# Output stage of a hybrid DeltaNet and attention layer: the residual gate moved from the weights to the results, and the first two units run side by side

## The chip, the cores and the metric

One core of a Trainium2 chip runs the whole layer. The metric is the device time of one execution in microseconds (us). TensorE (PE) multiplies, VectorE (DVE), ScalarE (ACT) and GpSimd (POOL) do the elementwise work, and SyncE (SP) and ScalarE issue the DMAs.

## The reference, cut to what matters

```python
def _merge(ya, yb, ga, gb, w_proj_a, w_proj_b, w_out):
    y = jax.nn.sigmoid(ga) * (ya @ w_proj_a) + jax.nn.sigmoid(gb) * (yb @ w_proj_b)
    return y @ w_out

def _layer(...):
...
    x = x + gate[:, None] * _merge(ya, yb, ga, gb, w_proj_a, w_proj_b, w_out)
```

`x` is 2048 x 1024, `w_out` is 1024 x 1024, and `gate` is one number for each of the 1024 output columns. The change touches the last product, `y @ w_out`, its gate and the residual.

## The kernel before

The kernel goes through the layer in stages: norms and modulation, input projections, the DeltaNet scan, attention with the branch projections beside it, and the output stage. A scheduler orders the stages before the last one. In the last one most engines run in the order in which the code is written (`manual_schedule`).

**The last projection.** `project(pj, wp, 3)` (L1218) is the fourth of four groups of 512 tokens. Each of its 16 PSUM tiles `pps` takes 12 matmuls. VectorE multiplies a tile by its branch gate (L1237: `ta`, `tb`), adds the two (L1239), and SyncE stores the sum to `ysp` (L1240). `ta` and `tb` have two buffers each, so a load waits for the store before it.

**The output stage** computes 256 tokens by 1024 columns at a time: eight units `u`, the first six from groups that were stored long before. A unit and `w_out` are each cut into 2 x 2 blocks (A11 to A22, B11 to B22), and seven products P1 to P7 replace the usual eight, with sums S1 to S4 of A blocks and T1 to T4 of B blocks (`OPS`). Every operand is split into a rounded `h` part and a rest `l`, and a product is 12 matmuls of 128 x 128 by 128 x 512: `h*h`, `h*l`, `l*h` for four slices (L1407 to L1414). Eight PSUM banks (`acc`) take the results in turn.

**The weights.** A gate row `gbc` is loaded from `gsp`, a block of `w_out` (1 MB) is loaded on ScalarE's queue (L1304) and multiplied by it (L1306), then cast to `h` (ScalarE) and rest `l` (VectorE or GpSimd). The next block's load stands behind the cast of the one before. T1 to T4 and their parts are made in steps 0 to 2 of the loop.

**The loop** (L1428) goes over the 56 products in the order unit by unit. At step `k` it writes the `l` part of the operand of product `k+4` (`los`, L1366: VectorE, but GpSimd for A22), the sums for `k+6` (L1349 to L1357: S3 and S1 on GpSimd, S2 and S4 on VectorE), the `h` part for `k+5` (`his`, ScalarE), the product `k`, and the results of `k-1`. Each of the seven left operands has one buffer.

**The results** (`outputs`). P1 is copied by ScalarE; P2 + P1 is output block 00; P6 adds to P1 (L1393) and P7 to that (L1394); P5 and P3 give blocks 11 and 01 (L1398 to L1401); P4 gives 10 (L1404). `store` (L1379) adds the residual `xr` on GpSimd, for the last unit on VectorE, and SyncE writes it out. P3 and P7 hold their PSUM banks until P5 and P6 are read.

Of the kernel before, what the change touches and what calls it, by code (L numbers as in the profile page):

```python
# [40 lines left out]
def _hybrid(ctx, tc, nc, V, S, G, T, ins, out, dbg, upto):  # L41
# [1158 lines left out]
    def load_y(pool, gi):  # L1200

        yy = []
        for src, po, tags in ((yasp, wq, ("wh", "wl")), (ybsp, pool, ("ybh", "ybl"))):
            hs, ls = [], []
            for k in range(4):
                if k % 2 == 0:
                    yh = po.tile([128, 2, 512], F32R, name="yh", tag=tags[0])
                    yl = po.tile([128, 2, 512], F32R, name="yl", tag=tags[1])
                yr = wq.tile([128, 512], F32, name="yr", tag="wr", bufs=2)
                dma(yr, src[gi][k])  # L1210
                S.copy(yh[:, k % 2], yr)
                V.tensor_tensor(yl[:, k % 2], yr, f32(yh[:, k % 2]), op=ALU.subtract)
                hs.append(yh[:, k % 2])
                ls.append(yl[:, k % 2])
# [37 lines left out]
    wp = []  # L1252
# [20 lines left out]

    EN = mybir.EngineType
    hpools.pop().__exit__(None, None, None)
    with tc.tile_pool(name="p4h", bufs=1, side="right", reuse_waits="tile") as hr, \
# [3 lines left out]
        units = [(gi, j * 256) for gi in (1, 2, 0, 3) for j in range(2)]  # L1280
        BH = lambda pool, nm: pool.tile([128, 4, 512], F32R, name=nm)
        AH = lambda pool, nm: pool.tile([128, 4, 128], F32R, name=nm, tag=nm)
# [3 lines left out]
        hi = {nm: BH(po, nm + "h") for nm, po in home.items()}  # L1286
        lo = {"B11": BH(er, "B11l")}
        A = {nm: [AH(po, nm + x) for x in "hl"] for nm, po in (("A11", el), ("A12", er))}
        ypool = lambda j, nm: p4 if j or nm == "A22" else el if nm == "A11" else er

        def load_quad(u, nm):
            gi, o = units[u]
            r, c = int(nm[1]) - 1, int(nm[2]) - 1
            if u == 0 and nm == "A22":
                t = wq.tile([128, 4, 128], F32, name="yq", tag="wr", bufs=2)
            else:
                t = ypool(u % 2, nm).tile([128, 4, 128], F32, name=f"y{nm}", tag=f"y{nm}{u % 2}")
            adma(t, ysp[gi][:, c * 4:c * 4 + 4, o + r * 128:o + r * 128 + 128])
            return t

        def scaled(nm, g, eng):
            i, j = int(nm[1]) - 1, int(nm[2]) - 1
            t = B[nm]
            adma(t, ins["w_out"][0, i * 512:i * 512 + 512, j * 512:j * 512 + 512].rearrange("(k p) c -> p k c", p=128))  # L1304
            for k in range(0, 4, 2):
                eng.tensor_tensor(t[:, k:k + 2], t[:, k:k + 2], g.unsqueeze(1).to_broadcast([128, 2, 512]), op=ALU.mult)  # L1306

        def gate_row(j):
            g = wq.tile([128, 512], F32, name="gbc", tag="wr", bufs=2)
            adma(g, gsp[:, j * 512:j * 512 + 512].to_broadcast([128, 512]))  # L1310
            return g

        Y = {}
        with tc.high_priority(tc.cur_priority - p_last), \
                tc.manual_schedule(engines={EN.DVE, EN.Activation, EN.Pool}):
            g0 = gate_row(0)
            scaled("B11", g0, V)
            S.copy(hi["B11"], B["B11"])
            scaled("B21", g0, V)
            V.tensor_tensor(lo["B11"], B["B11"], f32(hi["B11"]), op=ALU.subtract)  # L1320
            S.copy(hi["B21"], B["B21"])
            g1 = gate_row(1)
            scaled("B22", g1, V)
            S.copy(hi["B22"], B["B22"])
            scaled("B12", g1, G)
            V.tensor_tensor(B["B12"], B["B22"], B["B12"], op=ALU.subtract)
            S.copy(hi["B12"], B["B12"])
            for nm in ("A11", "A12", "A21", "A22"):
                Y[0, nm] = load_quad(0, nm)
            for nm in ("A11", "A12"):  # L1330
                S.copy(A[nm][0], Y[0, nm])
                V.tensor_tensor(A[nm][1], Y[0, nm], f32(A[nm][0]), op=ALU.subtract)

        for nm in ("B21", "B22", "T3"):
# [3 lines left out]
        for nm in ("S4", "S3", "S2", "S1", "A22"):  # L1338
            A[nm] = [AH(p4 if nm == "A22" else hr, nm + x) for x in "hl"]
        hi["T3"] = hi["B12"]  # L1340
        OPS = {"P1": ("A11", "B11"), "P2": ("A12", "B21"), "P3": ("S4", "B22"), "P7": ("S3", "T3"),
               "P6": ("S2", "T2"), "P5": ("S1", "T1"), "P4": ("A22", "T4")}
        seq = [(u, nm) for u in range(8) for nm in OPS]

        def sums(u, nm):

            y = lambda n: Y[u, n]
            if nm == "P2":
                G.tensor_tensor(y("A21"), y("A11"), y("A21"), op=ALU.subtract)  # L1349
                s2 = wq.tile([128, 4, 128], F32, name="s2", tag="wr", bufs=2)  # L1350
                V.tensor_tensor(s2, y("A22"), y("A21"), op=ALU.subtract)
                Y[u, "S3"], Y[u, "S2"] = y("A21"), s2
            if nm == ("P7" if u else "P3"):
                V.tensor_tensor(y("A12"), y("A12"), y("S2"), op=ALU.subtract)
                Y[u, "S4"] = y("A12")
            if nm == "P7":
                G.tensor_tensor(y("A11"), y("S2"), y("A11"), op=ALU.add)  # L1357
                Y[u, "S1"] = y("A11")

        def his(u, nm):  # L1360
            a = OPS[nm][0]
            S.copy(A[a][0], Y[u, a])

        def los(u, nm):
            a = OPS[nm][0]
# [147 lines left out]
```

## Time and profile before

| | us |
|---|---|
| median of 3 runs (lowest, highest) | 2032.99 (2029.52, 2043.38) |
| the profiled execution, and its span | 2029.11, 2027.3 |
| TensorE busy in the span | 1925.3 (95%) |
| VectorE, ScalarE, GpSimd busy | 1491.7, 808.7, 691.4 |
| mean granted TensorE clock | 0.979 |

In the rows of a timeline the first number is the start in us from the start of the span, the second the length, then engine, line, operation and tiles (output <- inputs); `x2` merges two that follow each other, and the brackets at the end give the idle time ahead and what ended it. ACTq and SPq are the times at which these engines issue a DMA. A line is one of the kernel before.

### The profile page before, as it was taken

To read this page: it belongs to the slowest core of one execution; us is meant where nothing else is said; L and a number is where in the kernel's file an instruction comes from. 1 tells how busy PE (TensorE), PEld (TensorE's weight loads), DVE (VectorE), ACT (ScalarE), POOL (GpSimd) and SP (SyncE) were. 2 spreads that over 40 slices of the span, in tenths; PEclk is the share of its full clock that TensorE was granted. 3 is DMA by queue.
4 is the path that set the end of the run, shared out by engine and by line. 5 is a ranking of instruction groups with operands and counts; after the bars stand their busy time and mean duration, and the time that the engine had idled before them with its cause. 6 is when DMAs were issued, how large, how long until landed. Compare 5 with 4: busy or idle time off the path is not lost. (4 is left out here: it accounts for less than half of the span.)

```text
span 2027.3 us, 32098 instructions
## 1 busy us (share of the span) xinstructions
PE 1925.3 (95%) x10947; PEld 1613.4 (80%) x10947; DVE 1491.7 (74%) x2850; ACT 808.7 (40%) x1998; POOL 691.4 (34%) x764
## 2 busy tenths in 40 slices
PE   7999999989999999999999999999899999995898
PEld 3888888779998778787888888888678888873787
DVE  7979766667776999999778775536777777656765
ACT  5755545554443322111222233325765555412221
POOL 1642211224542211014222333323654444304553
PEclk8999999999999999999999999999999999996999
DMA  7552326755447533537987787663555555363453
GB/s 258 165 141 89 95 86 164 189 150 164 147 139 196 163 110 114 141 91 227 248 248 213 222 236 218 172 194 119 191 174 155 183 156 169 105 211 94 150 171 115
DMA packets 387975, 333.12 MB, mean 164 GB/s; under 512 B 84136, under 2 KB 307680, under 8 KB 387172
## 3 DMA queue, kind: packets, MB, share of 16 engines
q1 hardware_dynamic: 352100, 288.07, 49.2%
q10 hardware_dynamic: 35712, 43.00, 6.1%
q8 instruction: 87, 1.43, 0.3%
q14 instruction: 76, 0.62, 0.1%
HBM read 220.28 MB, written 109.13 MB: 162 GB/s over the span
## 5 line engine op out<-in xcount | busy, mean ns | idle before, releaser
L524 PE MATMUL rps<-hh,wh 128*128 128x512 f32 x768 | 308.7, 402 | 5.7 <-DVE rt L818 4.5
L526 PE MATMUL rps<-hh,wl 128*128 128x512 f32 x768 | 308.4, 402 | 0.0
L525 PE MATMUL rps<-hl,wh 128*128 128x512 f32 x768 | 306.4, 399 | 0.0
L563 DVE SCALAR_TENSOR_TENSOR cacc<-y,cw,cacc 128x512 f32<-128x512 f32 (+1 forms) x224 | 162.3, 746 | 22.6 <-ACT cacc L561 18.4
L524 PEld LDWEIGHTS rps<-hh,wh 128*128 128x128 f32 x768 | 145.1, 189 | 40.3 <-DVE rt L818 5.0
L524 PE MATMUL lps<-hh,wh 128*128 128x512 f32 (+1 forms) x448 | 171.5, 383 | 0.3 <-ACT y L634 0.3
L525 PE MATMUL lps<-hl,wh 128*128 128x512 f32 (+1 forms) x448 | 171.3, 382 | 0.0
L526 PE MATMUL lps<-hh,wl 128*128 128x512 f32 (+1 forms) x448 | 171.3, 382 | 0.0
L526 PEld LDWEIGHTS rps<-hh,wl 128*128 128x128 f32 x768 | 145.0, 189 | 32.6
L525 PEld LDWEIGHTS rps<-hl,wh 128*128 128x128 f32 x768 | 145.1, 189 | 32.4
L945 DVE TENSOR_TENSOR pl<-pt,ph 128x512 fp32r<-128x512 f32 x156 | 105.5, 686 | 42.6 <-ACT ph L943 41.7
L943 ACT CAST ph<-pt 128x512 fp32r<-128x512 f32 x156 | 90.2, 585 | 111.4 <-PE pt L941 77.4
L917 DVE CUSTOM_DVE_ANT_0 pr<-sc,band,sk 128x640 f32<-128x640 f32 (+1 forms) x128 | 106.7, 863 | 33.1 <-PE sc L913 17.2
L816 ACT ACTIVATE rt<-rps 128x512 f32<-128x512 f32 x96 | 57.2, 596 | 181.9 <-PE rps L526 167.7
L747 DVE TENSOR_TENSOR btmp<-N 128x62 f32<-128x62 f32 (+30 forms) x124 | 116.9, 943 | 3.1
L927 POOL TENSOR_SCALAR pr<-pr,sm 128x640 f32<-128x640 f32 (+1 forms) x128 | 99.3, 795 | 56.7 <-DVE sm L925 39.8
L749 DVE TENSOR_TENSOR N<-N,btmp 128x62 f32<-128x62 f32 (+30 forms) x124 | 115.3, 930 | 3.0
L919 ACT ACTIVATE pr<-pr,sm 128x640 f32<-128x640 f32 (+1 forms) x128 | 104.0, 815 | 20.2 <-DVE sm L917 20.1
L246 DVE TENSOR_TENSOR wl<-wr,wh 128x512 fp32r<-128x512 f32 x120 | 93.2, 790 | 25.0 <-POOL wh L245 22.2
L1229 PE MATMUL pps<-yh,wph 128*128 128x512 f32 x256 | 105.1, 412 | 3.3 <-DVE tb L1237 1.8
L245 POOL TENSOR_SCALAR wh<-wr 128x512 fp32r<-128x512 f32 x72 | 48.1, 681 | 167.3 <-PE lps L525 67.5
L1230 PE MATMUL pps<-yl,wph 128*128 128x512 f32 x256 | 101.0, 396 | 0.0
(379 smaller groups left out, 5041.1 us busy)
## 6 DMA issues: line engine op xcount, KB each, us to landing
wr<-in_w_in_dram SPq DMA_DIRECT2D x120, 256.0 KB
kw<-Ksp SPq DMA_DIRECT2D x28, 384.0 KB
x<-vsp SPq DMA_DIRECT2D x36, 256.0 KB
k<-ksp SPq DMA_DIRECT2D x34, 256.0 KB
kT<-kTsp SPq DMA_DIRECT2D x34, 256.0 KB
wm<-in_w_mod_dram SPq DMA_DIRECT2D x16, 512.0 KB
xt<-in_x_dram SPq DMA_DIRECT2D x16, 512.0 KB
dtl<-Dsp SPq DMA_DIRECT2D x32, 256.0 KB
```

The source lines that it names most:

```text
L524: T.matmul(ps, lhsT=wh[:, k], rhs=xh[:, k], start=k == 0, stop=False)
L525: T.matmul(ps, lhsT=wh[:, k], rhs=xl[:, k], start=False, stop=False)
L526: T.matmul(ps, lhsT=wl[:, k], rhs=xh[:, k], start=False, stop=k == kt - 1)
L563: V.scalar_tensor_tensor(a, y[:, t:t + n], cw[:, m, t:t + 1], a, op0=ALU.mult, op1=ALU.add)
L747: V.tensor_tensor(tv, A[:, m + 1:, m].unsqueeze(2).to_broadcast([h1 + n, r, m]), A[:, m, 0:m].unsqueeze(1).to_broadcast([h1 + n, r, m]), o ...
L749: V.tensor_tensor(A[:, m + 1:, 0:m], A[:, m + 1:, 0:m], tv, op=ALU.add)
L917: V.tensor_tensor_reduce(s_, ps[:, o:768], band[:, b0:b0 + W + 256], -0.125, sk[:, 1, hd:hd + 1], ALU.add, ALU.min, sm[:, h, 1:2])
L919: S.activation(s_, s_, AF.Exp, scale=-1.0, bias=sm[:, h, 1:2], accum_out=sm[:, h, 2:3])
L927: G.tensor_scalar(p[:, h, :W + 256], p[:, h, :W + 256], sm[:, h, 3:4], 1.0, op0=ALU.mult, op1=ALU.mult)
L945: V.tensor_tensor(pl, pt, f32(ph), op=ALU.subtract)
L1229: T.matmul(ps, lhsT=wh[:, k, ms], rhs=hs[k], start=k == 0, stop=False)
L1230: T.matmul(ps, lhsT=wh[:, k, ms], rhs=ls[k], start=False, stop=False)
```

## The change

The gate is no longer multiplied into `w_out`. One row `gbc` of 1024 columns is kept, and `store` multiplies each result block by it ahead of the residual: on VectorE for blocks 11 and 01, on GpSimd for 00 and 10 (on VectorE in units 0 and 7 for some). In unit 7, P4 is gated straight from PSUM and its other half ahead of it.

The four blocks of `w_out` and three blocks of `y` are loaded in one row on ScalarE's queue, behind the cast of the third of four `yr` pieces of the last projection (`issue_after`), and their first parts are made behind the fourth. The 14 products of units 0 and 1 go in pairs (P1 of 0, P1 of 1, P2 of 0, ...); units 2 to 7 follow one by one. The left operands have six pairs of buffers that are used in turn. The loads of `x` follow their stores one by one (`load_x(j + 4)`). T1 is made on GpSimd, T2 on VectorE ahead of the loop, and the sums S2 of units 0 and 1 on GpSimd.

```diff
-        def scaled(nm, g, eng):
-            i, j = int(nm[1]) - 1, int(nm[2]) - 1
-            t = B[nm]
-            adma(t, ins["w_out"][0, i * 512:i * 512 + 512, j * 512:j * 512 + 512].rearrange("(k p) c -> p k c", p=128))
-            for k in range(0, 4, 2):
-                eng.tensor_tensor(t[:, k:k + 2], t[:, k:k + 2], g.unsqueeze(1).to_broadcast([128, 2, 512]), op=ALU.mult)
...
+        seq = [(u, nm) for nm in OPS for u in range(2)] + [(u, nm) for u in range(2, 8) for nm in OPS]
+        NP = 6
...
+        def load_w(nm):
+            i, j = int(nm[1]) - 1, int(nm[2]) - 1
+            adma(B[nm], ins["w_out"][0, i * 512:i * 512 + 512, j * 512:j * 512 + 512].rearrange("(k p) c -> p k c", p=128))
...
+        def pair(k):
+            j = k % NP
+            A[k] = [(el, er, hr)[min(j, 2)].tile([128, 4, 128], F32R, name=f"a{x}", tag=f"a{j}{x}") for x in "hl"]
...
+            with tc.issue_after(last["yh", 2].ins):
+                load_w("B11")
+                load_quad(0, "A11")
+                load_quad(1, "A11")
+                load_w("B22")
+                load_w("B12")
+                load_w("B21")
+                load_quad(0, "A12")
+            with tc.issue_after(last["yh", 3].ins), tc.issue_after(last["yl", 3].ins):
+                S.copy(hi["B11"], B["B11"])
+                split_lo("B11", V)
+                for k in range(2):
+                    his(k)
+                    los(k)
+                S.copy(hi["B22"], B["B22"])
+                V.tensor_tensor(B["B12"], B["B22"], B["B12"], op=ALU.subtract)
+                S.copy(hi["B21"], B["B21"])
+                V.tensor_tensor(B["B11"], B["B12"], B["B11"], op=ALU.add)
+                S.copy(hi["T3"], B["B12"])
...
+        def store(u, q, t, eng):
+            xr, dst, gate, j = X.pop((u, q))
+            eng.tensor_tensor(t, t, gate, op=ALU.mult)
             (V if u == 7 else G).tensor_tensor(xr, t, xr, op=ALU.add)
             dma(dst, xr)
+            load_x(j + 4)
...
+            split_lo("B21", V)
+            his(2)
+            for q in ((0, "A21"), (0, "A22"), (1, "A12"), (1, "A21"), (1, "A22")):
+                load_quad(*q)
...
+                elif k == 7:
+                    for nm in ("A11", "A12", "A21"):
+                        load_quad(2, nm)
+                elif k == 8:
+                    load_quad(2, "A22")
+                if k + 6 < len(seq):
+                    u, nm = seq[k + 6]
+                    if u > 1 and nm == "P2":
+                        s3(u)
+                        s2(u, V)
+                    elif u > 1 and nm == "P7":
+                        s4(u)
+                        s1(u)
```

Three places show how the change moves instructions. In the names `ah` and `al` are the parts of a left operand, numbers are buffers, and the brackets name the counters that an instruction waits for: an engine's, or one of the eight DMA queue counters, which each DMA waits for until the DMA before it on the same counter has landed.

**The start of the stage on ScalarE.** Before, from the cast of the last block of weights on:

```order
L1327 CAST B12h_19486<-B12_19482 128x2048 [waits DMAHW6_49,DMAHW4_49,DVE_49]
L1298 DMA yA11_19516<-ysp1_134 128x4x128 [waits DMAHW5_49,DMAHW2_49]
L1298 DMA yA12_19518<-ysp1_134 128x4x128 [waits DMAHW3_49]
L1298 DMA yA21_19520<-ysp1_134 128x4x128 [waits DMAHW4_49]
L1298 DMA yq_19522<-ysp1_134 128x4x128 [waits DMAHW5_49]
L1331 CAST A11h_19488<-yA11_19516 128x512 [waits DMAHW2_49]
L1331 CAST A12h_19490<-yA12_19518 128x512 [waits DMAHW3_49]
```

And now, where yA12_19498 and yA12_19538 are the A12 of units 0 and 1 (left operands of P2):

```order
L1345 CAST B12h_19486<-B12_19482 128x2048 [waits DVE_49]
L1319 CAST ah_19517<-yA12_19498 128x512 [waits DMAHW7_49,PE_49]
L1304 DMA yA21_19534<-ysp1_134 128x4x128 [waits DMAHW3_49,PE_49,Activation_49]
L1304 DMA yA22_19536<-ysp1_134 128x4x128 [waits DMAHW6_49]
L1304 DMA yA12_19538<-ysp1_134 128x4x128 [waits DMAHW0_49,PE_49,Activation_49]
L1304 DMA yA21_19540<-ysp1_134 128x4x128 [waits DMAHW2_49]
L1304 DMA yA22_19542<-ysp1_134 128x4x128 [waits DMAHW4_49]
L1319 CAST ah_19519<-yA12_19538 128x512 [waits DMAHW0_49]
```

Five loads now stand ahead of the cast for P2 of unit 1; the DMA ahead of the last one on its counter (DMAHW4) is the store of the last projected row.

**The start of the stage on VectorE.** Before, from the last two rows of the projection on:

```order
L1326 TENSOR_TENSOR B12_19482<-B22_19481,B12_19482 128x2048 [waits DMAHW1_49,Pool_49]
L1237 SCALAR_TENSOR_TENSOR ta_19442<-ta_19442,pps_19429 128x512 [waits DMAHW6_49,DMAHW0_49,PE_49]
L1237 SCALAR_TENSOR_TENSOR tb_19458<-tb_19458,pps_19445 128x512 [waits DMAHW7_49,PE_49]
L1239 TENSOR_TENSOR ta_19442<-ta_19442,tb_19458 128x512 [waits DVE_49]
L1332 TENSOR_TENSOR A11l_19489<-yA11_19516,A11h_19488 128x512 [waits DMAHW2_49,Activation_49]
```

And now:

```order
L1237 SCALAR_TENSOR_TENSOR tb_19458<-tb_19458,pps_19445 128x512 [waits DMAHW7_49,PE_49]
L1309 TENSOR_TENSOR B21l_19516<-B21_19480,B21h_19484 128x2048 [waits Activation_49]
L1323 TENSOR_TENSOR al_19518<-yA12_19498,ah_19517 128x512 [waits Activation_49]
L1239 TENSOR_TENSOR ta_19442<-ta_19442,tb_19458 128x512 [waits DVE_49]
L1323 TENSOR_TENSOR al_19520<-yA12_19538,ah_19519 128x512 [waits DMAHW0_49,Activation_49]
L1309 TENSOR_TENSOR B22l_19525<-B22_19481,B22h_19485 128x2048
L1366 TENSOR_TENSOR yA12_19498<-yA12_19498,s2_19556 128x512 [waits DVE_49,Pool_49]
L1323 TENSOR_TENSOR al_19522<-yA12_19498,ah_19521 128x512 [waits Activation_49]
L1366 TENSOR_TENSOR yA12_19538<-yA12_19538,s2_19562 128x512 [waits Pool_49]
```

The parts of P1 moved ahead of the projection's last rows, those of P2 (B21l) stand between them, and the projection's last sum behind B21l.

**The change from the pair to unit 2 on VectorE.** Before, around the same adds of unit 0 (`s2` is there that of unit 1):

```order
L1351 TENSOR_TENSOR s2_19620<-yA22_19589,yA21_19587 128x512 [waits DMAHW6_49,Pool_49]
L1389 TENSOR_TENSOR og_19636<-P2_19596,hold_19609 128x512 [waits DMAHW1_49,PE_49]
L1366 TENSOR_TENSOR A11l_19489<-yA11_19583,A11h_19488 128x512 [waits DMAHW3_49,Activation_49]
L1366 TENSOR_TENSOR A12l_19491<-yA12_19585,A12h_19490 128x512 [waits DMAHW4_49,Activation_49]
L1354 TENSOR_TENSOR yA12_19585<-yA12_19585,s2_19620 128x512 [waits DVE_49]
L1366 TENSOR_TENSOR S4l_19536<-yA12_19585,S4h_19535 128x512 [waits PE_49,Activation_49]
L1393 TENSOR_TENSOR hold_19609<-P6_19661,hold_19609 128x512 [waits PE_49]
```

And now, where s2_19760 is S2 of unit 2 and the lines after it read P6 and P7 of unit 0:

```order
L1323 TENSOR_TENSOR al_19684<-yA11_19491,ah_19683 128x512 [waits PE_49,Activation_49]
L1323 TENSOR_TENSOR al_19701<-yA11_19493,ah_19700 128x512 [waits PE_49,Activation_49]
L1363 TENSOR_TENSOR s2_19760<-yA22_19740,yA21_19721 128x512 [waits DMAHW5_49,DVE_49,Pool_49]
L1406 TENSOR_TENSOR hold_19604<-P6_19745,hold_19604 128x512 [waits PE_49]
L1407 TENSOR_TENSOR hold_19604<-P7_19703,hold_19604 128x512 [waits DVE_49]
```

With all eight banks taken by the pair, S2 of the next unit stands ahead of the add that empties P6's bank.

More of the change, by code (lines that the diff above doesn't have):

```diff
@@ L1335, in _hybrid @@
+        lo["B21"] = BH(hr, "B21l")
+        for k in range(2, NP):
+            pair(k)
+        for nm in ("B22", "T3"):
             lo[nm] = BH(hr, nm + "l")
@@ new lines, in s1, with load_x @@
+        def s1(u):
+            G.tensor_tensor(Y[u, "A11"], Y[u, "S2"], Y[u, "A11"], op=ALU.add)
+            Y[u, "S1"] = Y[u, "A11"]
+        R, held = {}, {}
+        outs = [(u, q) for u, nm in seq for q in {"P2": ["00"], "P5": ["11", "01"], "P4": ["10"]}.get(nm, [])]
+        X = {}
+        def load_x(j):
+            if j < len(outs):
+                u, q = outs[j]
+                gi, o = units[u]
+                r, c = int(q[0]), int(q[1])
+                rows = slice(gi * 512 + o + r * 128, gi * 512 + o + r * 128 + 128)
+                xr = p4.tile([128, 512], F32, name="xr", bufs=4)
+                dma(xr, ins["x"][0, rows, c * 512:c * 512 + 512])
+                X[u, q] = xr, out[0, rows, c * 512:c * 512 + 512], gbc[:, c * 512:c * 512 + 512], j
```

215 lines of the change are left out of this document (91 added, 124 removed).

## The prediction

> **What bounds the kernel now.** I read the windows of the last 130 us first (columns: stretch, its length, then busy time of PE, PEld, DVE, ACT, POOL, granted clock, DMA share, GB/s), then TensorE's timeline for the idle times, then the other engines' timelines for what ended them. All of the change lies after 1786 us; before it nothing moves.
>
> ```profile
> 1800.00:1850.00 50.00, 28.80 (x112) 22.45 (x112) 31.38 (x32) 8.16 (x7) 10.55 (x4) 0.81 0.64 215
> 1850.00:1900.00 50.00, 39.02 (x133) 29.52 (x132) 34.42 (x29) 14.44 (x19) 28.09 (x14) 0.78 0.31 90
> 1905.23:1924.70 19.47, 19.47 (x85) 15.78 (x84) 12.92 (x16) 4.74 (x9) 10.59 (x8) 1.00 0.52 161
> ```
>
> From 1900 on the output stage is dense at full clock: a unit of seven products takes 19.46 us, one product 2.78. The hundred microseconds before are not. TensorE's rows (start, length, then in brackets the idle time ahead and what ended it):
>
> ```profile
> 1836.68 0.80 PE L1412 MATMUL P<-B11h,A11h 128*128 128x512 f32 x1 [14.02 <-ACT A11h L1331]
> ...
> 1849.24 0.79 PE L1413 MATMUL P<-B21l,A12h 128*128 128x512 f32 x1 [7.17 <-DVE B21l L1419]
> ...
> 1881.42 0.79 PE L1414 MATMUL P<-T4h,A22l 128*128 128x512 f32 x1 [5.43 <-POOL A22l L1366]
> ...
> 1885.79 0.39 PE L1412 MATMUL P<-B11h,A11h 128*128 128x512 f32 x1
> ...
> 1905.23 0.40 PE L1412 MATMUL P<-B11h,A11h 128*128 128x512 f32 x1
> ...
> 2021.80 0.39 PE L1414 MATMUL P<-T4h,A22l 128*128 128x512 f32 x1
> ```
>
> The last projection matmul ends at 1836.68 - 14.02 = 1822.66, and the third unit (unit 2) starts at 1905.23: 82.6 us for two units that need 38.9. So 43.6 us is the most that the start can give. The first wait is for the weights:
>
> ```profile
> 1788.13 0.53 ACTq L1304 DMA_DIRECT2D B<-in_w_out_dram  x1
> 1798.68 0.39 ACTq L1304 DMA_DIRECT2D B<-in_w_out_dram  x1
> ...
> 1817.23 0.37 ACTq L1304 DMA_DIRECT2D B<-in_w_out_dram  x1
> 1796.28 2.36 DVE L1306 TENSOR_TENSOR B<-B,gbc 128x1024 f32<-128x1024 f32 x2 [7.34 <-DMA B<-in_w_out_dram]
> 1804.19 2.36 DVE L1306 TENSOR_TENSOR B<-B,gbc 128x1024 f32<-128x1024 f32 x2 [3.15 <-DMA B<-in_w_out_dram]
> ```
>
> Each block's load stands on ScalarE's queue behind a cast that waits for the block before. The second block took 1804.19 - 1798.68 = 5.5 us from issue to use.
>
> **The first products (gain).** Without the gates and with the loads in one row, the first block is issued at about 1787, and four blocks and three quarters of a megabyte of `y` need at most 4 x 5.5 = 22 us even if they overlap in nothing: B11 with its parts is ready before 1800, all by 1809, before 1822.66. The 14.02 us go, and both P1 run to 1822.66 + 5.6 = 1828.2. I cost the loads' share of the DMA at nothing: the projection's matmuls cover it through eight PSUM banks. Bound: its `ta` loads late by one block's 5.5 us.
>
> **What is late next.** Here the changed order decides (the rows of the order are above). The DVE rows for its steps:
>
> ```profile
> 1830.57 2.29 DVE L1326 TENSOR_TENSOR B<-B,B 128x2048 f32<-128x2048 f32 x1
> 1833.37 0.68 DVE L1237 SCALAR_TENSOR_TENSOR tb<-tb,pps 128x512 f32<-128x512 f32 x1
> 1841.47 4.79 DVE L1351 TENSOR_TENSOR s<-yq,yA 128x512 f32<-128x512 f32 x1 [3.21 <-DMA yq<-ysp]
> 1888.60 0.68 DVE L1404 TENSOR_TENSOR hold<-P,hold 128x512 f32<-128x512 f32 x1
> 1894.08 0.69 DVE L1351 TENSOR_TENSOR s<-yA,yA 128x512 f32<-128x512 f32 x1 [3.70 <-POOL yA L1349]
> 1903.28 0.68 DVE L1399 TENSOR_TENSOR hold<-P,hold 128x512 f32<-128x512 f32 x1
> 2023.45 0.69 DVE L1379 TENSOR_TENSOR xr<-hold,xr 128x512 f32<-128x512 f32 x1
> ```
>
> and POOL's:
>
> ```profile
> 1841.05 4.66 POOL L1419 TENSOR_TENSOR B22l<-B,B22h 128x2048 fp32r<-128x2048 f32 x1
> 1886.82 4.71 POOL L1379 TENSOR_TENSOR xr<-hold,xr 128x512 f32<-128x512 f32 x3 [3.76 <-DVE hold L1399]
> 1909.98 1.28 POOL L1349 TENSOR_TENSOR yA<-yA,yA 128x512 f32<-128x512 f32 x1
> ```
>
> DVE's `s` of 512 columns takes 0.69 at 1894.08 but 4.79 at 1841.47, where POOL's 4.66 us operation runs: it waited until 1845.7. The add from PSUM at 1888.60 takes its 0.68 inside POOL's three. So an operation of DVE with both inputs in SBUF and one of POOL exclude each other; those with PSUM do not. The Trainium skill (SBUF — State Buffer, Who interferes with whom) calls it an exclusive lock on a port pair, and its section on the two sides of SBUF says it is held for the whole instruction. It speaks against this change: a gate put on a result that lies in SBUF has two SBUF inputs and falls under the lock. By the rule the steady unit comes to the 21.2 us that are worked out below from rows, and the sum to 2027. Were the port shared instead, POOL's three turns and two `al` of that unit would overlap (21.2 - 3.75 - 1.2 = 16.3, under TensorE's 19.46) and the collisions of steps 3 and 4 would go: 2019 - 9 = 2010. I take the rule, since the rows agree.
>
> Step by step (a step of DVE is 0.60 for 512 columns, 0.71 if it uses the one just before; 2.2 for 2048; POOL 1.25 and 4.6; a cast 0.62):
> 1. B21l stands on DVE behind `tb` of the last projected row. That ended its start at 1833.97 and now lacks the 2.29 of L1326 ahead of it: 1831.7, so B21l is there at 1834.0. P2 of unit 0 waits 5.8 us. Bounds: 1831 to 1836.3.
> 2. ScalarE loads five `y` blocks ahead of the cast for P2 of unit 1; each issue waits for its queue counter, the last for the store of the last projected row, whose add now follows B21l (1834.6 + 0.7). A store there took 1804.87 - 1800.46 = 4.4 from its issue to the load that waits for it:
>
> ```profile
> 1800.46 0.32 SPq L1240 DMA_DIRECT2D ysp<-ta  x1
> ...
> 1804.87 1.62 SPq L1236 DMA_DIRECT2D ta<-gasp  x2
> ```
>
>    1834.7 + 0.6 + 4.4 and the cast: P2 of unit 1 at about 1840. No wait of this kind shows in the trace, so the bounds are 1834.7 (none) and 1841.
> 3. DVE: `al`, B22l (2.2), S4; cast; P3 of unit 0 starts about 1844. POOL, once it has `s2` of unit 1 (its block lands 3.9 after its issue, 1843; then 1.25), starts T1 (4.6) at about 1845.7, in the way of unit 1's S4: 1850.3, cast, `al`: P3 of unit 1 at 1852.
> 4. T3l (2.2, to 1856.2), then POOL's T4 takes the port to 1860.8; `al` of S3: P7 of unit 0 runs from 1861.5 at low clock to 1865.5. Bound for 3 and 4: no collision, 2 x 4.6 less.
> 5. Five products of 2.78 follow: 1879.5.
> 6. P4 of unit 0 takes the bank of P6 of unit 0, which DVE's L1406 frees; L1406 stands behind `s2` of unit 2, which needs the A22 block that is loaded after POOL's T4l (4.6, to 1879.0) and `al` (1.25). A load takes 3.9 (below, from the first issue to the second block's cast); `s2` and L1406: 1885.6. So TensorE waits 6.1 us, and starts at low clock as in the row at 1881.42, which stays at it until 1885.5 (below): +1.6. Unit 2 starts at 1885.6 + 4.3 + 2.8 = 1892.7.
>
> ```profile
> 1832.95 1.49 ACTq L1298 DMA_DIRECT2D yA<-ysp  x3
> ...
> 1836.92 0.62 ACT L1331 CAST A12h<-yA 128x512 fp32r<-128x512 f32 x1 [0.29 <-DMA yA<-ysp]
> 1885.43 0.52 PE L1414 MATMUL P<-T4h,A22l 128*128 128x512 f32 x1
> 1823.72 4.63 POOL L1306 TENSOR_TENSOR B<-B,gbc 128x1024 f32<-128x1024 f32 x2 [43.18 <-DMA B<-in_w_out_dram]
> ```
>
> Against 1905.23 the start gains 12.5 us, not 43.6. With the bounds: 8 to 27.
>
> **The later units (loss).** The gates on the weights go (three pairs of 2.36 on DVE, 4.63 on POOL, all before the stage and counted there), and each unit gets four gates on its results instead: two on DVE, two on POOL. In a unit DVE has a chain that closes over POOL: s2, og, two `al`, S4, `al`, L1406, L1407, `al`, two of P5, P3's add, two gates: 14 x 0.60 = 8.4; between them POOL's gate, xr and S1 take their turns: 3.75; then POOL's two xr, gate, xr, `al`, S3 (the next s2 waits for it): 7.5, with two `al` of DVE between: 1.2; four dependent steps: 0.4. Sum 21.2 against TensorE's 19.46. The same chain now: 11 x 0.60 + 2 x 1.25, then three xr, `al`, S3 = 6.25, and two `al`: 16.6, and it shows idle time (the 3.70 at 1894.08, and POOL's 3.76 at 1886.82). The lead of some 4 us at unit 2 uses up in two units; the next four lose 1.75 each and the last `al` half a microsecond: 7.5. Bounds: 0, if the turns overlap, and 5 x 1.75 = 8.8 plus as much again if every turn costs 0.2 more.
>
> **The end (loss).** From the last matmul's end (2022.2) to the end of DVE's last (2024.14) are 1.9 us. Unit 7 now has nine steps instead of five after P5, with the gates: 9 x 0.60 and five dependences, then two for P4: DVE ends about 4.5 after TensorE, +2.6. Bounds 1 to 3.
>
> **Sum.** -12.5 + 7.5 + 2.6 = -2.4. The profiled execution took 2029.1 (span 2027.3), below the runs' median of 2033.0 and at the low end of 2029.5 to 2043.4. 2029.1 - 2.4 = 2026.7; I say 2027.
>
> **Rivals.**
> - *The pairing works:* no wait after the P1, -43.6 + 2.6: 1988. Against it: steps 1 and 6, which the order shows. 3%.
> - *Half of it works:* no collision in 3 and 4, no bank wait in 6 (7.7), and the loop does not bind: -12.5 - 7.7 - 4.6 + 2.6 = -22: 2007. 7%.
> - *The loop does not bind* while the start goes as above: -12.5 + 2.6: 2019. For it: the turns may overlap more than I add up; against it: the rows at 1841.47 and 1894.08 fit the exclusion to a tenth. 18%.
> - *Slower:* the loop costs more, since each turn between DVE and POOL costs both. POOL's three xr above took 4.71 instead of 3.75 with one turn; nine at 1.6 instead of 1.25 give 24.4 a unit, 5 x 4.9 = 25 instead of 7.5: +15, 2044; at 25.5 a unit it passes +1%. It is slower than now from 21.9 a unit on (10 us over four to five units). 9%, half of it beyond +1%.
> - *The loads collide:* 4.75 MB in a row beside the projection's `ta` and `tb` make its banks late by up to 5.5: 2032. 5%.
>
> My forecast, within a few us of now, holds the other 58%. A measurement of this kernel tells about 1% (20 us) from no change. Faster by more than that are the first two: 0.10. Slower: 0.05. Within 1%: 0.85. The range takes the bounds of the start (15 below) and of the loop (9 above) and the spread of the runs (2043 is the highest now): 2012 to 2042.
>
> **What would show it.** Right: P1 of unit 0 follows the projection at about 1823; TensorE waits before P2 (about 6 us, for B21l) and before P4 of unit 0 (about 6, for DVE); unit 2 starts near 1893; from unit 4 on units of 21 us with a short wait in P6; DVE's last some 4.5 us after TensorE's. Wrong: P2 without a wait, a dense stage from unit 2 to the end (19.46 each), or a projection that ends after 1826.

## The result, and the profile after

| | before | changed |
|---|---|---|
| median of 6 runs | 2034.49 us (2029.52 to 2043.38) | 2023.83 us (2018.68 to 2025.93) |
| ratio to before | | 0.9941, 95% interval 0.9916 to 0.9966 |
| span of the profiled execution | 2027.3 us | 2019.4 us |

The changed kernel is faster by 0.6%, about 11 us. The forecast was 2027 us with a range of 2012 to 2042, and the likeliest case "within 1%"; all of that held. How much of this was luck is said behind the experiments. The rest of this part shows where the gain stands and where it was lost.

Two executions differ by a few us in parts of the program that the change does not touch, so lengths are counted from a common point: the start of TensorE's last matmul of the projection that waits for DVE's `tb` before the output stage begins. The first row below is that point in the kernel before, the others are TensorE's rows of the changed kernel (start, length, in brackets the idle time ahead and what ended it).

```profile
1777.59 0.51 PE L1229 MATMUL pps<-yh,wph 128*128 128x512 f32 x1 [1.81 <-DVE tb L1237]
```

```profile
1780.55 0.51 PE L1229 MATMUL pps<-yh,wph 128*128 128x512 f32 x1 [1.63 <-DVE tb L1237]
1796.27 0.97 PE L1229 MATMUL pps<-yh,wph 128*128 128x512 f32 x3 [1.45 <-ACT yh L1211]
...
1827.24 0.39 PE L1434 MATMUL P<-B11h,ah 128*128 128x512 f32 x1
...
1835.25 0.50 PE L1435 MATMUL P<-B21l,ah 128*128 128x512 f32 x1 [2.08 <-DVE B21l L1309]
1839.99 0.50 PE L1434 MATMUL P<-B21h,ah 128*128 128x512 f32 x1 [1.53 <-ACT ah L1319]
1844.17 0.50 PE L1434 MATMUL P<-B22h,ah 128*128 128x512 f32 x1 [0.87 <-ACT ah L1319]
1851.98 0.79 PE L1434 MATMUL P<-B22h,ah 128*128 128x512 f32 x1 [4.49 <-ACT ah L1319]
1861.23 0.78 PE L1436 MATMUL P<-B12h,al 128*128 128x512 f32 x1 [2.97 <-DVE al L1323]
1884.67 0.77 PE L1434 MATMUL P<-T4h,ah 128*128 128x512 f32 x1 [5.51 <-DVE hold L1406]
...
1982.32 0.50 PE L1436 MATMUL P<-T2h,al 128*128 128x512 f32 x1 [0.30 <-DVE al L1323]
2002.68 0.50 PE L1436 MATMUL P<-T2h,al 128*128 128x512 f32 x1 [0.38 <-DVE al L1323]
...
2011.14 0.40 PE L1436 MATMUL P<-T4h,al 128*128 128x512 f32 x1
```

P1 of unit 0 follows the projection without a gap (1827.24); the 14.02 us of before are gone. In their place stand six shorter waits in units 0 and 1, each where the prediction's steps put one, and a wait of 1.45 in the projection that they do not name. In a second profile of the same kernel (below) five of the six stand in the same places; the wait for the cast of P2 of unit 1 is missing there, and TensorE waits 1.2 us for an `al` of P2 instead. The windows of the changed kernel (columns as in the prediction) show the same stretch, then two of the later units:

```profile
1800.00:1850.00 50.00, 42.92 (x178) 32.53 (x176) 31.84 (x34) 8.72 (x7) 9.23 (x5) 1.00 0.62 199
1850.00:1900.00 50.00, 39.54 (x143) 30.99 (x144) 39.72 (x37) 13.69 (x20) 32.38 (x16) 0.83 0.27 84
1892.10:1911.48 19.38, 19.38 (x85) 15.78 (x84) 14.24 (x17) 2.88 (x5) 15.05 (x11) 1.00 0.68 218
...
1969.89:1990.31 20.42, 20.04 (x86) 15.62 (x84) 14.53 (x19) 4.43 (x8) 13.85 (x9) 1.00 0.52 157
```

From 1800 to 1850 TensorE is now busy 42.9 us at full clock instead of 28.8 at 0.81. From 1850 to 1900 little has changed: 39.5 instead of 39.0. (Both windows are counted from the span's start, and the common point lies 3.0 us later in this trace.) Unit 2 starts at 1892.10 and takes 19.38; unit 6 takes 20.42, of which TensorE is idle for 0.4: there another engine sets the pace.

From the common point, with the last matmul's end at 2011.14 + 0.40, the 10.86 us come from three terms:

| from the common point, us | before | changed | difference | predicted |
|---|---|---|---|---|
| start of unit 2 | 127.64 | 111.55 | -16.09 | -12.5 |
| units 2 to 7 | 116.96 | 119.44 | +2.48 | +7.5 |
| last matmul's end to the end of the span | 5.11 | 7.86 | +2.75 | +2.6 |
| end of the span | 249.71 | 238.85 | -10.86 | -2.4 |

### The profile page after: what moved, and what is told of

Read it like the earlier page. It is cut to its first block, busy times and chain, and to the rows that moved or that the text cites. A ratio compares the mean times of both kernels' runs of the same rounds, so it can differ in the third digit from the quotient of the medians.

```text
span 2019.4 us, 32107 instructions
## 1 busy us (share of the span) xinstructions
PE 1923.7 (95%) x10947; PEld 1611.3 (80%) x10947; DVE 1501.3 (74%) x2863; ACT 807.4 (40%) x1998; POOL 713.7 (35%) x776
## 5 line engine op out<-in xcount | busy, mean ns | idle before, releaser
L524 PEld LDWEIGHTS rps<-hh,wh 128*128 128x128 f32 x768 | 145.3, 189 | 39.5 <-DVE rt L818 4.0
L1231 PE MATMUL pps<-yh,wpl 128*128 128x512 f32 x256 | 100.9, 396 | 0.0
```

Of the source, the lines that this page charges most:

```text
L524: T.matmul(ps, lhsT=wh[:, k], rhs=xh[:, k], start=k == 0, stop=False)
L1231: T.matmul(ps, lhsT=wl[:, k, ms], rhs=hs[k], start=False, stop=k == 3)
```

## The experiments

Each kernel is one edit of the changed kernel unless it says otherwise. All lengths are from the common point of its own trace. The changed kernel was profiled a second time beside the experiments:

> The changed kernel itself beside the others on the same chip: 0.994 of the kernel before, 238.9 from the common point.

It came to 238.6 against 238.9, where the runs' times scatter by several us. The start of unit 2 differs by more, 0.7 us. With this one repetition to go by, I read nothing into differences under 0.5 us at the end and 1 us at unit 2.

| kernel | start of unit 2 | last matmul's end | end of span | ratio to before, 95% interval |
|---|---|---|---|---|
| changed | 111.55 | 231.0 | 238.9 | 0.9941 (0.9916 to 0.9966) |
| changed, again | 112.26 | 230.7 | 238.6 | 0.9959 (0.9944 to 0.9975) |
| 1 gates left out | 109.53 | 226.1 | 230.9 | 0.9911 (0.9889 to 0.9933) |
| 2 P6's adds ahead of `s2` | 106.74 | 230.4 | 238.4 | 0.9952 (0.9934 to 0.9969) |
| 3 both | 104.35 | 221.0 | 225.8 | 0.9897 (0.9876 to 0.9919) |
| 4 T1, T4 on DVE | 107.47 | 226.0 | 233.9 | 0.9931 (0.9913 to 0.9950) |
| 5 the units' steps on DVE | 110.31 | 226.9 | 234.5 | 0.9924 (0.9899 to 0.9948) |
| 6 all on DVE, P6's adds ahead | 101.33 | 219.6 | 227.1 | 0.9885 (0.9859 to 0.9911) |
| 7 as 6, units 0 and 1 not paired | 106.66 | 223.2 | 230.9 | one run |
| 8 changed, not paired | 118.99 | 235.6 | 243.3 | one run |
| 9 loads behind the fourth cast | 111.81 | 231.6 | 239.5 | one run |
| 10 cast ahead of the loads | 114.13 | 233.6 | 241.5 | one run |
| 11 last add ahead of B21l | 111.32 | 230.6 | 238.5 | one run |

**1, 2 and 3: what the gates cost, and what a visible wait is worth.** Experiment 1 leaves the four gate products out:

```diff
-            eng.tensor_tensor(t, t, gate, op=ALU.mult)
...
-                    V.tensor_tensor(held[u][:, 1], held[u][:, 1], gate, op=ALU.mult)
...
-                V.tensor_tensor(held[u][:, 0], ps, gate, op=ALU.mult)
-                V.tensor_tensor(xr, held[u][:, 0], xr, op=ALU.add)
+                V.tensor_tensor(xr, ps, xr, op=ALU.add)
```

> The changed kernel with the four gate products of each output unit left out (the output is x plus the ungated sum). All lengths are counted from TensorE's wait for the projection's tb (1780.55 in the changed kernel's trace) to the end of the span: 249.7 before, 238.9 changed. Theory (DVE and POOL close a loop of 20.4 us a unit, which holds TensorE from unit 4 on): without two gates on DVE (1.2) and two on POOL (1.7 each) the loop is 15.8, under TensorE's 19.34, so the later units take 19.34 each (-2.5), unit 7's steps after the last product are fewer (-2.5), and POOL reaches T4l 1.7 sooner (-1.7): 232, 6.7 less than the changed kernel. Rival (the gates lie beside other work, something else holds the units): only the last unit's gates show, 236.

230.9: 7.9 less than the changed kernel. Unit 2 starts 2.0 sooner, units 2 to 7 take 116.6 instead of 119.4, and the end after the last matmul is 4.8 instead of 7.9. The next two fences are DVE's `s2` of two units in a row, without the gates and then in the changed kernel:

```profile
1932.65 0.69 DVE L1363 TENSOR_TENSOR s<-yA,yA 128x512 f32<-128x512 f32 x1 [3.70 <-POOL yA L1358]
...
1949.86 0.69 DVE L1363 TENSOR_TENSOR s<-yA,yA 128x512 f32<-128x512 f32 x1 [3.70 <-POOL yA L1358]
```

```profile
1968.65 0.69 DVE L1363 TENSOR_TENSOR s<-yA,yA 128x512 f32<-128x512 f32 x1 [5.05 <-POOL yA L1358]
...
1989.02 0.69 DVE L1363 TENSOR_TENSOR s<-yA,yA 128x512 f32<-128x512 f32 x1 [5.06 <-POOL yA L1358]
```

The loop is 17.2 us without gates (while DVE catches up with TensorE, which needs 19.34) and 20.4 with them; it was expected to shrink to 15.8. In both, DVE stands idle ahead of `s2` until POOL has done `S3`: the idle time is a part of the loop, not spare time. The first expectation held (232 expected), the rival did not (236).

Experiment 2 issues `s3` and `s2` of unit 2 one product later, behind the adds L1406 and L1407 that free the bank which P4 of unit 0 waits for:

```diff
-                    if u > 1 and nm == "P2":
+                    if u == 2 and nm == "P3":
+                        outputs(k - 1)
+                        s3(u)
+                        s2(u, V)
+                    elif u > 2 and nm == "P2":
...
-                if k:
+                if k and k != 10:
                     outputs(k - 1)
```

> The changed kernel with s3 and s2 of unit 2 issued one product later, behind the two adds that free the bank of P6 of unit 0. Theory: the wait of 5.5 us before P4 of unit 0 goes, with the 1.6 of low clock after it, so unit 2 starts about 7 us sooner (104.5 after the common point instead of 111.5); but s2 of unit 2 still stands at the landing of its A22 block, and the loop of DVE and POOL starts there, so TensorE waits it back in units 2 to 7 and the end moves by 0 to -2: 237 to 239 instead of 238.9. Rival (that wait is worth what it lasts): -7, 232.

The wait of 5.51 us, the longest in the changed kernel, is gone, and unit 2 starts 4.8 sooner (7 were expected). The end moves by 0.5, hardly more than two profiles of one kernel differ. TensorE's waits in this kernel:

```profile
1862.48 0.79 PE L1436 MATMUL P<-B12h,al 128*128 128x512 f32 x1 [3.54 <-DVE al L1323]
1897.49 0.50 PE L1436 MATMUL P<-B12h,al 128*128 128x512 f32 x1 [1.60 <-DVE al L1323]
1920.22 0.50 PE L1436 MATMUL P<-T2h,al 128*128 128x512 f32 x1 [0.30 <-DVE al L1323]
...
2001.71 0.50 PE L1436 MATMUL P<-T2h,al 128*128 128x512 f32 x1 [0.38 <-DVE al L1323]
```

Nothing waits between 1862 and 1897 any more, but unit 2 now waits itself, and then every unit from 3 on, where the changed kernel had its first such wait in unit 6. TensorE starts earlier into a loop that runs no sooner.

> Both edits together: gates left out, and s3 and s2 of unit 2 behind the two adds of P6. Theory: with the loop short, the wait that goes before P4 counts now: -6.7 - 7 = -13.7, 225, much more than the two alone (-6.7 and about -1). Rival (the two are independent): the sum of the two single results, whatever these are.

Both edits together give 225.8: 13.1 less, against 7.9 and 0.5 alone. The edit of experiment 2 is worth 5.1 (230.9 - 225.8) once the loop of DVE and POOL has been shortened, and 0.5 at most as long as it has not. Not all of the 5.1 is the wait: without gates it lasts only 2.45 us. Behind it both P4 take 7.20 us at a granted clock of 0.76, and 5.56 at 1.00 in kernel 3, which is another 1.6. The last 1.2 stand ahead of it, where the products from P7 of unit 0 on take 19.06 at 0.85 without the edit and 17.85 at 0.90 with it; nothing in the edit explains these. For the end all three expectations of the theory held within 1.1 us; the start of unit 2 in experiment 2 missed by 2.2.

**4: T1 and T4 on DVE.**

```diff
-            G.tensor_tensor(B["B22"], B["B22"], B["B11"], op=ALU.subtract)
+            V.tensor_tensor(B["B22"], B["B22"], B["B11"], op=ALU.subtract)
...
-                    G.tensor_tensor(B["B21"], B["B21"], B["B11"], op=ALU.subtract)
+                    V.tensor_tensor(B["B21"], B["B21"], B["B11"], op=ALU.subtract)
```

> The changed kernel with the two weight sums T1 and T4 (128x2048 each) on DVE instead of POOL. Theory (an operation of DVE and one of POOL with both inputs in SBUF exclude each other): S4 of unit 1 took 5.00 and the al of S3 5.02 because they stood behind POOL's 4.5 and 6.6; now they stand behind 2.2 each, so P3 of unit 1 and P7 of unit 0 wait some 2 to 3 us less each, POOL is free for what follows, and the end comes 2 to 6 us sooner: 233 to 237 instead of 238.9. Rival (port shared, an operation costs its own time wherever it runs): DVE has 4.4 us more work in the stretch where TensorE waits for it: 239 to 243.

233.9, 5.0 less. First the changed kernel's rows of the collision (DVE's S4 of unit 1 and the `al` of S3, POOL's T1 and T4), then the same steps of DVE in experiment 4:

```profile
1846.28 5.00 DVE L1366 TENSOR_TENSOR yA<-yA,s 128x512 f32<-128x512 f32 x1 [1.44 <-POOL s L1363]
...
1856.17 5.02 DVE L1323 TENSOR_TENSOR al<-yA,ah 128x512 fp32r<-128x512 f32 x1
1846.19 4.53 POOL L1457 TENSOR_TENSOR B<-B,B 128x2048 f32<-128x2048 f32 x1
...
1854.05 6.58 POOL L1474 TENSOR_TENSOR B<-B,B 128x2048 f32<-128x2048 f32 x1
```

```profile
1842.54 2.29 DVE L1457 TENSOR_TENSOR B<-B,B 128x2048 f32<-128x2048 f32 x1
...
1846.41 1.76 DVE L1366 TENSOR_TENSOR yA<-yA,s 128x512 f32<-128x512 f32 x1
...
1851.99 0.68 DVE L1323 TENSOR_TENSOR al<-yA,ah 128x512 fp32r<-128x512 f32 x1
```

S4 falls from 5.00 to 1.76 and the `al` from 5.02 to 0.68, with T1 now done by DVE itself in 2.29. POOL's T4 took 6.58 where T1 took 4.53: POOL waits for DVE just as DVE for POOL. Giving DVE 4.6 us more work made the kernel faster, which the rival excluded.

**5 and 6: the same steps without POOL.** Experiment 5 puts every step of the units on DVE and leaves T1, T4, T4l and the first two `s2` on POOL; experiment 6 puts those on DVE too and adds the edit of experiment 2.

```diff
-            (G if nm == "P4" else V).tensor_tensor(A[k][1], ...
+            V.tensor_tensor(A[k][1], ...
...
-            (V if u == 7 else G).tensor_tensor(xr, t, xr, op=ALU.add)
+            V.tensor_tensor(xr, t, xr, op=ALU.add)
...
-            gp = V if u in (0, 7) else G
+            gp = V
```

(and `s1` and `s3` from `G` to `V` likewise).

> The changed kernel with every step of the units that stood on POOL (S3, S1, the al of P4, the gates and the adds of x) on DVE; T1, T4, T4l and the first two s2 stay on POOL. Lengths from TensorE's wait for the projection's tb to the end of the span (238.9 in the changed kernel). Theory (the turns between DVE and POOL cost more than the work): a unit is now 26 steps of 0.60 on DVE with some ten dependences of 0.11, 16.7 us, under TensorE's 19.34, so units 2 to 7 take 19.4 each (-2.5), and the al of P4 no longer stands behind T4l on POOL, so unit 2 starts 2 to 4 sooner; the steps after the last product were on DVE before: 232 to 235. Rival (DVE becomes the bound: 26 steps at the 0.69 that its rows show come to 17.9, and with its waits for casts pass 19.34): 239 or more.

234.5, as the theory had it. The window of unit 6 in this kernel:

```profile
1971.06:1990.51 19.45, 19.45 (x85) 15.77 (x84) 16.83 (x27) 4.83 (x8) 0.00 (x0) 1.00 0.50 162
```

DVE does in 16.8 us what DVE and POOL did in 14.5 and 13.9 with a loop of 20.4, and TensorE is never idle. Two things made that loop long, and no run separates them. In the one from 1968.65 to 1989.02 of the changed kernel DVE's steps are 3.9 us longer in all than the 0.69 each that they show elsewhere; and six steps of POOL, 8.9 us, stand between the gates of P5 and the end of `S3`, each of 1.25 or more where DVE needs 0.60. Unit 2's start was expected 2 to 4 sooner and came only 1.2 sooner (1.9 against the second profile): DVE now has a gate to do while POOL's T4l holds it off, and the gate and the `al` behind it make TensorE wait (TensorE's, DVE's and POOL's rows):

```profile
1877.25 0.80 PE L1436 MATMUL P<-T2h,al 128*128 128x512 f32 x1 [5.09 <-DVE al L1323]
...
1871.27 4.59 DVE L1389 TENSOR_TENSOR og<-og,gbc 128x512 f32<-128x512 f32 x1
...
1870.78 4.54 POOL L1309 TENSOR_TENSOR T4l<-B,T4h 128x2048 fp32r<-128x2048 f32 x1 [12.36 <-DVE T1l L1309]
```

> Everything of the output stage that stood on POOL moved to DVE (T1, T4, T4l and the first s2 too), and s3 and s2 of unit 2 behind the adds of P6; the gates stay on the results. Theory, if the edits' parts add: T1 and T4 on DVE -5.0 (as measured), the loop no longer binds -2.5, and with that the wait before P4 of unit 0 counts, -6 with the low clock behind it -1.6: about 224 instead of 238.9, some 15 us less than the changed kernel. Rival (DVE alone becomes late in the paired units, since it takes another 5 us of T4l and S-sums there): the gain of P6 is lost, 230 or more.

227.1, between the two: 3 more than the theory, 3 less than the rival. This is the fastest kernel of the study that computes everything, 0.9885 of the kernel before (2004.92 against 2029.51 us) where the changed kernel beside it has 0.9959 (2019.95). What is missing to 224 stands in good part in unit 2, which takes 21.0 (122.37 - 101.33 from the common point) instead of 19.4, and in a wait of 4.62 for P3 of unit 1 that is as long as before. TensorE's row in unit 2 and two of DVE's:

```profile
1885.18 0.50 PE L1436 MATMUL P<-B12h,al 128*128 128x512 f32 x1 [1.38 <-DVE al L1323]
...
1868.44 0.69 DVE L1406 TENSOR_TENSOR hold<-P,hold 128x512 f32<-128x512 f32 x1
...
1896.27 0.68 DVE L1370 TENSOR_TENSOR yA<-s,yA 128x512 f32<-128x512 f32 x1
```

Between the two rows of DVE, 1868.44 to 1896.95, its steps follow each other without an idle moment: the results of units 0 and 1 come out two by two, and with POOL's share on DVE its queue is full just when unit 2's operands are due. So the rival's mechanism is there. How the 3 us divide between it and that wait was not tried.

**7 and 8: what pairing by product is worth.** Both take the order of the first two units back to one after the other, with the steps that depend on it; 7 stands beside 6, 8 beside the changed kernel.

```diff
-        seq = [(u, nm) for nm in OPS for u in range(2)] + [(u, nm) for u in range(2, 8) for nm in OPS]
+        seq = [(u, nm) for u in range(8) for nm in OPS]
...
-                load_quad(1, "A11")
+                load_quad(0, "A12")
```

> The first two units one after the other again instead of paired by product, everything else of the change kept, and POOL's steps of the stage on DVE as in the run before (so that the later units do not bind). Theory: each new right operand is now wanted every 2.78 us instead of 5.56, while DVE and ScalarE make one in about 4; TensorE waits before more of the first seven products, unit 2 starts 5 to 9 us later than in the paired kernel of the run before, and the end as much: 229 to 233. Rival (pairing is worth nothing, the bound is the last rows of the projection): the same as the run before, 222 to 226.

> The changed kernel with the first two units one after the other instead of paired by product, nothing else changed. Theory (the loop of DVE and POOL sets the end): unit 2 starts some 6 us later (117 to 119 after the common point instead of 111.5), but the loop has less lag to work off and the end moves by 0 to +2 only: 239 to 241. Rival (pairing counts in full): +6, 245.

Beside kernel 6 unit 2 starts 5.3 later, as expected, and the end is 3.7 later (230.9): inside the expected 229 to 233, but less than unit 2's start, because unit 2 itself now takes 19.4 instead of 21.0. Beside the changed kernel unit 2 starts 7.4 later, but the end only 4.5 (243.3). Neither expectation of the last one held in full: I had let the loop take 4 to 6 of the 6, and it took 2.9 of 7.4, since unpaired units leave DVE less late and TensorE then runs units 2 to 7 in 116.6. TensorE's waits in kernel 8 are for one new right operand after another:

```profile
1863.15 0.80 PE L1434 MATMUL P<-T2l,ah 128*128 128x512 f32 x1 [5.54 <-DVE T2l L1309]
1870.66 0.50 PE L1434 MATMUL P<-T1l,ah 128*128 128x512 f32 x1 [2.16 <-DVE T1l L1309]
1878.40 0.78 PE L1434 MATMUL P<-T4l,ah 128*128 128x512 f32 x1 [3.13 <-POOL T4l L1309]
```

So of the 16.1 us that the start gained, 8.7 (127.64 - 118.99) come with the rest of the change (loads in a row, gates taken off the weights, rotating left operands, which were not tried apart), and 7.4 with the pairing, as far as this one order of the unpaired steps shows.

**9, 10 and 11: the start, step by step.** Experiment 9 issues the loads behind the fourth cast of the projection's `y`, 10 puts the cast for P2 of unit 1 ahead of four of five loads on ScalarE, 11 puts DVE's last add of the projection ahead of B21l.

```diff
-            with tc.issue_after(last["yh", 2].ins):
+            with tc.issue_after(last["yh", 3].ins):
```

> The changed kernel with the row of early loads issued behind the fourth cast of the projection's y instead of behind the third. Theory of the 1.45 us that TensorE waited for that cast in the projection: seven issues on ScalarE's queue stood ahead of it; without them the projection ends 1.5 to 1.8 sooner (44.9 to 45.2 after the common point instead of 46.7), and the products of units 0 and 1 follow by as much: 237. Rival (what the cast gains is lost again, since the 4.75 MB then collide with later loads of the projection's ta and tb): the projection ends sooner, the end is 239 to 241.

The projection ends 1.8 sooner and without the wait of 1.45, so the seven issues ahead of the cast were its cause. They take ScalarE's queue from 1789.62 to 1795.56 in the changed kernel, and the cast follows at once:

```profile
1795.60 0.62 ACT L1211 CAST yh<-yr 128x512 fp32r<-128x512 f32 x1 [5.37 <-issue]
```

But the end is 239.5, in the rival's range: B21l is waited for 4.51 instead of 2.08, and the products from P2 on come 0.6 later than in the changed kernel. TensorE was only early for what DVE could not give yet: DVE's steps for the last two `ta` of the projection wait for DMAs and come 1.6 and 0.5 later, as the rival has it.

```diff
-            for q in ((0, "A21"), (0, "A22"), (1, "A12"), (1, "A21"), (1, "A22")):
+            load_quad(1, "A12")
+            his(3)
+            for q in ((0, "A21"), (0, "A22"), (1, "A21"), (1, "A22")):
```

> The changed kernel with ScalarE's cast for P2 of unit 1 ahead of four of the five y loads that stood before it. Theory (the cast waited for a load's queue counter, not for its own data): the wait of 1.53 before P2 of unit 1 goes, but the loads for S4 come later by as much, P3 waits instead, and the end is the same within 1.5: 237.5 to 240. Rival (the wait counts): 237 or less, or, if the loads' delay is longer than what the cast gained, 241 and more.

241.5: the cast comes 9.5 us sooner (49.3 instead of 58.8), and the four loads behind it end their issue 3.4 later (62.1 instead of 58.7), by more than the 1.53 that TensorE no longer waits. Their data are the next to be missed: TensorE waits 2.71 and 6.27 for P3 instead of 0.87 and 4.49. ScalarE's rows in the changed kernel, then in this one:

```profile
1826.08 13.19 ACTq L1304 DMA_DIRECT2D yA<-ysp  x5
1839.32 0.62 ACT L1319 CAST ah<-yA 128x512 fp32r<-128x512 f32 x1 [14.29 <-DMA ysp<-ta]
```

```profile
1831.24 0.37 ACTq L1304 DMA_DIRECT2D yA<-ysp  x1
1835.30 0.63 ACT L1319 CAST ah<-yA 128x512 fp32r<-128x512 f32 x1 [5.10 <-DMA yA<-ysp]
1835.94 12.16 ACTq L1304 DMA_DIRECT2D yA<-ysp  x4
```

One such issue alone takes 0.37 us, five take 13.2, and the profile names the store of the projection's last row as what ended it. In the nine profiles of the study with this order on ScalarE and DVE the cast starts 3.6 us after DVE's last add of the projection (3.59 to 3.64), whether that add starts 53.6 or 55.9 after the common point. In experiment 10 the profile names another DMA, the load of `gbc`, as what ended the four issues.

```diff
+            with tc.issue_after(last["add", 7].ins):
+                split_lo("B21", V)
...
-            split_lo("B21", V)
```

> The changed kernel with DVE's last add of the projection (the one whose store ScalarE's loads of y wait for) ahead of B21l instead of behind B21l and an al. Theory (those loads and the cast behind them wait for that store): the store starts about 3 us sooner, ScalarE's cast for P2 of unit 1, at 58.8 after the common point in the changed kernel, comes at about 56, B21l comes 0.6 later, the waits before P2 of unit 1 and P3 of unit 0 go, and the end is 1 to 2 sooner: 237 to 238. Rival (the cast waits for the loads' own data or their number): the cast stays within 1 of 58.8 and the end at 238.5 to 240.

```profile
1825.11 11.82 ACTq L1304 DMA_DIRECT2D yA<-ysp  x5
1836.97 0.62 ACT L1319 CAST ah<-yA 128x512 fp32r<-128x512 f32 x1 [12.91 <-DMA ysp<-ta]
```

With the add earlier the same cast comes at 57.5 instead of 58.8, and the waits before P2 of unit 1 and P3 of unit 0 are gone: the mechanism is right (the first of these waits alone would not show it, since the second profile of the changed kernel lacks it too). The add came only some 1.8 us sooner, not 3, since an `al` ahead of it took 1.50 beside POOL's `s2`; and the end is 238.5, in the rival's range. P4 of unit 0 starts 1.1 sooner, but the P4 of units 0 and 1 take longer. Their windows, in the changed kernel and then in this one (the granted clock is the third value from the end):

```profile
1884.67:1892.10 7.43, 7.42 (x24) 5.93 (x25) 7.36 (x12) 1.66 (x3) 2.35 (x2) 0.74 0.00 0
```

```profile
1882.49:1890.79 8.30, 8.30 (x24) 6.58 (x25) 8.23 (x12) 1.72 (x3) 3.23 (x3) 0.65 0.00 0
```

The same 24 matmuls take 8.30 us at a granted clock of 0.65 instead of 7.43 at 0.74, which leaves 0.2 of the 1.1 at unit 2, and the loop takes that.

## Why the prediction was right, and where its sizes were off

**The waits and their causes were right.** Every wait of the paired units stands where the steps put it and has the cause that they name: B21l, the cast behind the loads (experiments 10 and 11), S4 and the `al` behind POOL's T1 and T4 (experiment 4), and P4 of unit 0 behind `s2` of unit 2 (experiment 2). The causes behind B21l itself and P3 of unit 0 are read from the order and the rows. The last wait was predicted at 6.1 us and is 5.51, and `s2` and L1406 stand as the step says:

```profile
1883.23 0.69 DVE L1363 TENSOR_TENSOR s<-yA,yA 128x512 f32<-128x512 f32 x1 [9.42 <-POOL yA L1358]
1883.85 0.68 DVE L1406 TENSOR_TENSOR hold<-P,hold 128x512 f32<-128x512 f32 x1
```

**The start: 16.1 instead of 12.5.** Counted from the common point, P3 of unit 1 was put at 74.4 and came at 71.4, unit 2 at 115.1 and came at 111.6: the error arises in steps 1 and 2 and is then carried along. Step 1 took DVE's last `tb` from the trace of before and took off only the 2.29 of L1326. It moved by more:

```profile
1831.42 0.68 DVE L1237 SCALAR_TENSOR_TENSOR tb<-tb,pps 128x512 f32<-128x512 f32 x1
1832.02 3.18 DVE L1309 TENSOR_TENSOR B21l<-B,B21h 128x2048 fp32r<-128x2048 f32 x1
...
1835.72 0.68 DVE L1239 TENSOR_TENSOR ta<-ta,tb 128x512 f32<-128x512 f32 x1
```

That `tb` starts 50.9 after the common point; before it was 55.8 (1833.37 - 1777.59), 4.9 later. With P1 1.6 later than I had it (the projection's wait of 1.45, which I did not foresee because I priced the loads' share of the DMA and not their issues ahead of a cast), the wait for B21l came to 2.08 instead of 5.8. B21l itself was put at 2.2 and takes 3.18, as POOL's first `s2` runs beside it (1.29 from 1831.76). Step 2 then put 4.4 us and an issue between the add and the cast; from 1835.72 + 0.68 to 1839.32 are 2.9. Of the 4.9 that `tb` gained, 3.1 stand ahead of L1326, in a `ta` that waits for its load: it starts 51.05 after the common point in the kernel before (first row) and 48.00 now (second row).

```profile
1828.64 0.69 DVE L1237 SCALAR_TENSOR_TENSOR ta<-ta,pps 128x512 f32<-128x512 f32 x1 [6.97 <-DMA ta<-gasp]
```

```profile
1828.55 0.69 DVE L1237 SCALAR_TENSOR_TENSOR ta<-ta,pps 128x512 f32<-128x512 f32 x1 [2.82 <-DMA ta<-gasp]
```

SyncE issues such a load once a store ahead of it has landed, and waited up to 5.0 us for one in the kernel before, 2.7 now. That the fourth block of `w_out`, which was being loaded at that time, made the store slow is argued, not shown.

**The later units: +2.5 instead of +7.5.** The mechanism was right (experiments 1, 3 and 5), the size was not. The loop was summed to 21.2 and is 20.4, so a bound unit costs some 1.1 us instead of 1.75. And the lead with which TensorE enters holds for three units instead of two: units 2 to 4 take 19.34 to 19.38, and only units 5 to 7 are longer. TensorE's own unit has also become 0.1 shorter in these (last section), which I could not expect.

**The end: +2.8 instead of +2.6.** DVE's last step ends 4.8 after the last matmul (2015.64 + 0.69 - 2011.54), against 4.5 predicted:

```profile
2015.64 0.69 DVE L1422 TENSOR_TENSOR xr<-hold,xr 128x512 f32<-128x512 f32 x1
```

Without the gates (experiment 1) the end after the last matmul is 3.1 shorter.

**How near the number came.** The forecast put -2.4 us on a base of 2029.1, the profiled execution. The profiles differ by -10.9 and the medians by -10.7, over four times as much, since the start and the later units both erred to the same side, by 3.6 and 5.0. That 2027 still lies 3 us from 2023.8 is luck: the median of the kernel before is 2034.5, 5.4 above the base.

**The rivals.** Pairing without any later wait was excluded by the trace as predicted. "The loop does not bind" came out half true: it binds, but for three units out of six. "The loop costs more" and "the loads collide" did not happen; the loads do cost 1.45 us in the projection, and experiment 9 shows that their removal alone gains nothing. Two sums among the prediction's terms do not agree: "half of it works" takes 4.6 off for the collisions of steps 3 and 4, while their bound and the rival with a shared port take 9 (with 9.2 it would be 2002). And step 4 names nothing that fills the time from 1852 to 1854, where its T3l starts.

## What to carry to other kernels

A wait that the trace shows is worth what the next limit leaves of it: taking away the longest wait here, 5.5 us, was worth 0.5 at most alone, and the same edit 5.1 together with a shorter loop of DVE and POOL, some 4 of it the wait of 2.45 left there and the low clock behind it. Sum the steps of the engines that close a loop, turns included, before moving work onto the less busy of them; where their operations exclude each other and one needs 1.25 us for what the other does in 0.60, the work may be quicker on one engine alone (26 steps on DVE in 16.8 us, against 20.4 on both). And where a load is issued on an engine that also computes, look at what stands behind it in the queue and at what the issue itself waits for.

## What the runs showed of the hardware

DVE and POOL exclude each other in both directions. In the changed kernel many of POOL's adds of `x` take 1.6 to 1.7 us beside DVE's steps, where it needs 1.25 to 1.3 alone, and its T4 6.58 instead of 4.5. The Trainium skill (Perfetto Trace Analysis, Optimizing Scalar/DVE Operations) says that offloading operations between these two might not help; in this stage it hurts, and taking T1 and T4 back from POOL gave 5.0 us.

TensorE's unit, at a granted clock of 1.00 in both kernels, takes 19.34 to 19.38 in units 2 to 4, against 19.46 before, though its 84 matmuls are the same. In the experiments whose units are not bound (1, 3, 5 to 8) units 5 and 6 take 19.44 to 19.49 again. What brings this was not tried.
